# A new order of 33 transfers instead of 39, and the transposes of the last four tiles moved off TensorE, in a matmul with scale and add

## The chip, the cores and the metric

One core of a Trainium2 chip. The metric is the device time of one execution in microseconds; lower is better. Spans quoted from profiles are about 1.8 us shorter than the device time of the same run.

## The reference

```
x: (16, 512, 1024) float32, weight: (1024, 768) float32, add_value: (16, 512, 768) float32, scale = 0.1
out = (scale * matmul(x, weight) + add_value).astype(float32)
```

The 16 x 512 rows of x are 64 tiles of 128 rows. A tile of x has 0.524 MB, a tile of addend or output 0.393 MB, and all data together are 87.03 MB.

## The kernel before

One queue, issued from SyncE, carries every transfer in the order of `STREAM`. An entry is (kind, first tile, tiles): `x` loads rows of x, `w` weights, `a` addends, `o` stores output, `l` and `r` store the left and right columns of a tile.

```
STREAM = [
    ("x", 0, 3), ("w", 0, 2), ("w", 2, 2), ("w", 4, 2), ("x", 3, 1), ("w", 6, 2),
    ("a", 0, 3), ("x", 4, 4), ("a", 3, 1), ("a", 4, 4), ("x", 8, 4), ("x", 12, 4),
    ("x", 16, 4), ("a", 8, 8), ("x", 20, 4), ("x", 24, 8), ("o", 0, 8), ("a", 16, 8),
    ("x", 32, 8), ("a", 24, 8), ("a", 32, 8), ("x", 40, 8), ("o", 8, 8), ("x", 48, 8),
    ...
X_SLOTS = 16      # tiles of x in SBUF at a time
A_SLOTS = 32      # addend tiles; the output is made in place
```

x is needed transposed. Early tiles are cast on GpSimd and transposed on TensorE. For the tiles of `MOVED_ACT` and `MOVED_POOL`, ScalarE or GpSimd moves a pair of tiles in 16 casting copies, and VectorE turns the pair with one stream transpose. Four consecutive pairs (one x load of eight tiles) alternate between the two engines, so each engine moves two pairs per load.

```
MOVED_ACT = [14, 18, 22, 26, 30, 34, 38, 42, 46, 50, 54, 58]
MOVED_POOL = [16, 20, 24, 28, 32, 36, 40, 44, 48, 52, 56]
...
        elif op == "x":
            if last >= X_SLOTS:
                while done["cast"] <= last - X_SLOTS:
                    step()                       # emits the work that frees the slots
            nc.sync.dma_start(xs[:, k:k + n, :], rows(x_v, s, n))
```

The load of x32-39 overwrites the slots of x16-23, so its issue waits until the pairs 16, 18, 20 and 22 are moved. SyncE issues in order: while this entry waits, nothing behind it is issued.

## Time and profile before

| | before |
|---|---|
| device time, median of 4 runs | 210.12 us (209.95 to 210.92) |
| profiled span | 208.5 us |
| packets on the queue | 5616 |
| longest waits of the issuer | for ScalarE's moves, 90.1 us in five waits |

The prediction shows the main lines. The view of what the issuer waited for has three more. The columns are waiting engine and line, what it waited for, and then microseconds in total, times, and the longest.

```profile
SPq L258 <- ACT va L118: 90.1, 5, 22.0
SPq L264 <- DMA out_dram<-ao: 40.1, 4, 23.2
SPq L272 <- DVE ao L185: 21.7, 8, 6.9
```

The issuer waits nearly all the time.

### The profile page before, as it was taken

The numbers are of one execution on the slowest core, as the hardware profiler recorded it, in microseconds if no ns is written. First come the engines' busy times: TensorE is split into PE (matmuls) and PEld (weight loads), VectorE is DVE, ScalarE is ACT, GpSimd is POOL, SyncE is SP. The second block draws the span as 40 slices with busy tenths as digits, with TensorE's granted clock in tenths as the row PEclk, the third lists the DMA queues.
The fourth block names the chain that finished last, engine by engine and source line by source line (L and its number), as shares of the span: only waits on it lengthen the run. The fifth ranks groups of instructions, "written<-read, shape, count | busy, mean of one in ns | idle before, by whom it ended". The sixth has DMA issues, their size and how long they took to land.

```text
span 208.5 us, 2886 instructions
## 1 busy us (share of the span) xinstructions
PE 181.6 (87%) x1096; PEld 110.7 (53%) x1096; DVE 101.3 (49%) x111; ACT 129.0 (62%) x206; POOL 124.3 (60%) x199
## 2 busy tenths in 40 slices
PE   0599399980899997999999999999999999989960
PEld 0455256650466664566666666666666666656630
DVE  0536535511466514855655555555553685233330
ACT  2423000499959798599999999999999900003210
POOL 1310524379898980999998899999999960001000
PEclk9999889996589999999999999999999999999997
DMA  6999999999999999999999999999999999999995
GB/s 236 415 428 440 413 429 434 421 450 406 454 418 448 407 429 462 404 443 420 442 434 413 461 418 424 420 429 437 421 434 424 432 439 424 429 418 439 429 394 214
DMA packets 5629, 87.21 MB, mean 418 GB/s; under 512 B 624, under 2 KB 752, under 8 KB 2032
## 3 DMA queue, kind: packets, MB, share of 16 engines
q1 hardware_dynamic: 5616, 87.03, 98.2%
q8 instruction: 8, 0.13, 0.3%
q14 instruction: 5, 0.04, 0.0%
HBM read 61.87 MB, written 25.17 MB: 417 GB/s over the span
## 4 chain that ended last, share of the span: by engine, by line
DMA 75%; ACT 9%; PE 7%; DVE 3%; SPq 1%; issue 1%; DVEq 0%
DMA out_dram<-ao 35%; DMA ao<-in_add_value_dram 22%; DMA xs<-in_x_dram 13%; ACT va L118 9%; PE mm L177 6%; DMA ao<-in_weight_dram 5%; DVE ao L185 2%; DVE xt L126 1%; PE tp L156 1%; SPq L258 1%; SPq L99 0%; SPq L264 0%; SPq L272 0%; DVEq L185 0%
## 5 line engine op out<-in xcount | busy, mean ns | idle before, releaser
L177 PE MATMUL mm<-w_bf,xt 128*128 128x256 bf16 (+1 forms) x1024 | 173.8, 331 | 8.8 <-DVE xt L164 6.6
L177 PEld LDWEIGHTS <-xt 128*128 128x128 bf16 x1024 | 101.3, 99 | 76.9 <-DVE xt L164 7.0
L118 ACT CAST va<-xs 32x512 bf16<-32x512 f32 x192 | 118.2, 616 | 28.8 <-DMA xs<-in_x_dram 19.1
L118 POOL CAST va<-xs 32x512 bf16<-32x512 f32 x176 | 106.8, 607 | 15.9 <-DVE xt L126 6.2
L185 DVE SCALAR_TENSOR_TENSOR ao<-mm,ao 128x768 f32<-128x768 f32 (+2 forms) x62 | 58.1, 942 | 78.1 <-PE mm L177 49.1
L146 POOL CAST xb<-xs 128x1024 bf16<-128x1024 f32 x15 | 15.2, 1040 | 43.4 <-PE tp L156 22.5
L164 ACT COPY xt<-tp 128x512 bf16<-128x512 bf16 (+1 forms) x11 | 8.2, 785 | 35.3 <-PE tp L156 35.3
L126 DVE STREAM_TRANSPOSE xt<-va 128x1024 f32<-128x1024 f32 x23 | 28.4, 1234 | 0.0
L156 PE MATMUL tp<-identity,xb 128*128 128x128 f32 x72 | 12.9, 314 | 11.2 <-DVE xb L142 7.4
L156 PEld LDWEIGHTS tp<-identity,xb 128*128 128x128 f32 x72 | 9.8, 161 | 13.7 <-issue 7.6
L164 DVE COPY xt<-tp 128x1024 bf16<-128x1024 bf16 x10 | 6.9, 686 | 10.1 <-PE tp L156 10.1
L101 DVE CAST w_bf<-ao 128x768 bf16<-128x768 f32 x8 | 4.1, 556 | 3.8 <-DMA ao<-in_weight_dram 3.8
L142 DVE CAST xb<-xs 128x512 bf16<-128x512 f32 x3 | 1.9, 696 | 6.8 <-DMA xs<-in_x_dram 6.8
L144 POOL CAST xb<-xs 128x512 bf16<-128x512 f32 x2 | 1.6, 834 | 5.5 <-DMA xs<-in_x_dram 5.5
L144 ACT CAST xb<-xs 128x512 bf16<-128x512 f32 x1 | 0.6, 618 | 4.8 <-DMA xs<-in_x_dram 4.8
L213 DVE TENSOR_SCALAR ao<-mm 128x768 f32<-128x768 f32 x2 | 1.8, 952 | 1.9 <-PE mm L177 1.9
L245 DVE TENSOR_TENSOR ao<-ao 128x768 f32<-128x768 f32 x3 | 2.7, 951 | 0.0
L144 ACT ACT_TABLE_LOAD x1 | 1.3, 1283 | 0.7 <-PEq L289 0.7
L210 ACT ACTIVATE ao<-mm 128x768 f32<-128x768 f32 x1 | 0.8, 817 | 0.0
masks.py:197 POOL MEMSET identity<- 128x128 f32 x1 | 0.2, 204 | 0.3 <-POOLq L289 0.3
masks.py:199 POOL TENSOR_SCALAR_AFFINE_SELECT identity<-identity 128x128 f32<-128x128 f32 x1 | 0.3, 292 | 0.1
L289 POOL MEMSET const-float32-0.0<- 128x1 f32 x1 | 0.1, 98 | 0.2 <-issue 0.2
(3 smaller groups left out, 0.3 us busy)
## 6 DMA issues: line engine op xcount, KB each, us to landing
ao<-in_add_value_dram SPq DMA_DIRECT2D x7, 3072.0 KB, 26.1
out_dram<-ao SPq DMA_DIRECT2D x7, 3072.0 KB, 23.9
xs<-in_x_dram SPq DMA_DIRECT2D x5, 4096.0 KB, 18.8
xs<-in_x_dram SPq DMA_DIRECT2D x5, 2048.0 KB, 26.6
ao<-in_weight_dram SPq DMA_DIRECT2D x4, 768.0 KB, 9.6
xs<-in_x_dram SPq DMA_DIRECT2D x1, 1536.0 KB, 6.1
ao<-in_add_value_dram SPq DMA_DIRECT2D x1, 1536.0 KB, 19.3
out_dram<-ao SPq DMA_DIRECT2D x1, 1536.0 KB, 12.9
```

The lines of the kernel that those rows point to most:

```text
L101: nc.vector.tensor_copy(w_bf[:, j + i, :], ao[:, s + i, :])
L118: move(moved[t0][32 * b:32 * b + 32, :, a, :], src[32 * a:32 * a + 32, :, b, :])
L126: nc.vector.transpose(xt.rearrange("p i c m -> p (i c m)"), moved.pop(t0).bitcast(fp32).rearrange("p c a k -> p (c a k)"))
L142: nc.vector.tensor_copy(xb[:, 0:K // 2], src[:, 0:K // 2])
L144: other(xb[:, K // 2:K], src[:, K // 2:K])
L146: nc.gpsimd.tensor_copy(xb, src)
L156: nc.tensor.transpose(tp[:, c, :], pairs[:, c * P:(c + 1) * P], identity)
L164: evacuate(xt_tiles[t][:, c:c + q, :].bitcast(bf16), tp[:, c:c + q, :].bitcast(bf16))
L177: nc.tensor.matmul(mm_tiles[t, cols[0]][:, n0:n1], lhs(t, j), w_bf[:, j, n0:n1], start=(j == 0), stop=(j == KJ - 1))
L185: nc.vector.scalar_tensor_tensor(a, mm_tiles[t, part][:, n0:n1], float(scale), a, op0=mybir.AluOpType.mult, op1=mybir.AluOpType.add)
L245: nc.vector.tensor_add(ao[:, t, :], ao[:, EARLY_AT + t, :], ao[:, t, :])
L258: nc.sync.dma_start(xs[:, k:k + n, :], rows(x_v, s, n))
```

## The change

Its intent: fewer and larger transfers, no transposes on TensorE near the end, and a last store that waits for no arithmetic of its own. The diff, cut to its core:

```
     ("x", 0, 3), ("w", 0, 2), ("w", 2, 2), ("w", 4, 2), ("x", 3, 1), ("w", 6, 2),
-    ("a", 0, 3), ("x", 4, 4), ("a", 3, 1), ("a", 4, 4), ("x", 8, 4), ("x", 12, 4),
-    ("x", 16, 4), ("a", 8, 8), ("x", 20, 4), ("x", 24, 8), ("o", 0, 8), ("a", 16, 8),
-    ("x", 32, 8), ("a", 24, 8), ("a", 32, 8), ("x", 40, 8), ("o", 8, 8), ("x", 48, 8),
-    ("a", 40, 8), ("o", 16, 8), ("x", 56, 8), ("a", 48, 8), ("o", 24, 8), ("o", 32, 8),
-    ("a", 56, 8), ("o", 40, 8), ("o", 48, 8), ("o", 56, 4), ("o", 60, 1), ("o", 61, 1),
-    ("o", 62, 1), ("l", 63, 1), ("r", 63, 1),
+    ("x", 4, 4), ("a", 0, 8), ("x", 8, 8), ("a", 8, 8), ("x", 16, 8), ("a", 16, 8),
+    ("o", 0, 8), ("x", 24, 8), ("x", 32, 8), ("a", 24, 8), ("o", 8, 8), ("x", 40, 8),
+    ("a", 32, 8), ("o", 16, 8), ("a", 40, 8), ("x", 48, 8), ("x", 56, 8), ("a", 48, 8),
+    ("o", 24, 8), ("o", 32, 8), ("a", 56, 8), ("o", 40, 8), ("o", 48, 8), ("o", 56, 6),
+    ("l", 63, 1), ("r", 63, 1), ("o", 62, 1),
...
-MOVED_ACT = [14, 18, ..., 54, 58]
-MOVED_POOL = [16, 20, ..., 52, 56]
+MOVED_ACT = [14, 18, ..., 54, 58, 62]
+MOVED_POOL = [16, 20, ..., 52, 56, 60]
...
-        evacuate = nc.scalar.copy if t <= EARLY or t > LAST_PAIR else nc.vector.tensor_copy
+        evacuate = nc.scalar.copy if t <= EARLY else nc.vector.tensor_copy
```

The weight loads get another form of the same view, with the same rows.

More of the change, by code (lines that the diff above doesn't have):

```diff
@@ L26 @@
 EARLY = 3
-MOVED_ACT = [14, 18, 22, 26, 30, 34, 38, 42, 46, 50, 54, 58]
-MOVED_POOL = [16, 20, 24, 28, 32, 36, 40, 44, 48, 52, 56]
+MOVED_ACT = [14, 18, 22, 26, 30, 34, 38, 42, 46, 50, 54, 58, 62]
+MOVED_POOL = [16, 20, 24, 28, 32, 36, 40, 44, 48, 52, 56, 60]
 @with_exitstack
@@ L67, in rows @@
         return view[:, s // G, s % G:s % G + n, :]
-    w_v = weight.rearrange("(c p r) n -> p c r n", p=P, r=2)
+    w_v = weight.rearrange("(c p r) n -> p c (r n)", p=P, r=2)
     const = ctx.enter_context(tc.tile_pool(name="const", bufs=1))
@@ L95, in load_w @@
         s = A_SLOTS - KJ + j
-        if n == 1:
-            nc.sync.dma_start(ao[:, s, :], w_v[:, j // 2, j % 2, :])
-        else:
-            nc.sync.dma_start(ao[:, s:s + 2, :], w_v[:, j // 2, :, :])
+        assert j % 2 == n % 2 == 0
+        nc.sync.dma_start(
+            ao[:, s:s + n, :].rearrange("p (c r) n -> p c (r n)", r=2),
+            w_v[:, j // 2:(j + n) // 2, :])
         for i in range(n):
@@ L216, in head @@
             done["step"] = EARLY
-    LAST_PAIR = max(in_pair)
     EARLY_AT = A_SLOTS - KJ - EARLY
@@ L259 @@
             done["x"] = s + n
-            if last < EARLY:
+            if s < EARLY:
                 head(op, s, n)
```

## The prediction

> **What bounds the kernel now.** I read the page first, for the share of each engine and of the transfers (parts 1 to 4).
>
> ```profile
> PE 181.6 (87%) x1096; PEld 110.7 (53%) x1096; DVE 101.3 (49%) x111; ACT 129.0 (62%) x206; POOL 124.3 (60%) x199
> DMA  6999999999999999999999999999999999999995
> DMA packets 5629, 87.21 MB, mean 418 GB/s; under 512 B 624, under 2 KB 752, under 8 KB 2032
> q1 hardware_dynamic: 5616, 87.03, 98.2%
> ```
>
> All data move on one queue whose packets fill 98.2% of the 16 engines' time. Idle is 1.8% of 208.5 us = 3.75 us, and only the first and last slices are not full. To find what the busy time is worth, I asked for the windows (busy time of each engine, then PE clock, DMA share, GB/s):
>
> ```profile
> 4.00:16.00 12.00, 8.30 (x45) 5.57 (x46) 5.35 (x10) 3.74 (x7) 2.66 (x3) 1.00 1.01 420
> 88.00:156.00 68.00, 68.00 (x421) 40.96 (x420) 40.27 (x41) 66.25 (x108) 62.77 (x105) 1.00 1.00 430
> 198.00:205.00 7.00, 3.58 (x23) 1.90 (x20) 2.07 (x3) 0.73 (x1) 0.00 (x0) 1.00 0.96 398
> 205.00:206.00 1.00, 0.00 (x0) 0.00 (x0) 0.00 (x0) 0.00 (x0) 0.00 (x0) 0.80 0.72 280
> 206.00:207.00 1.00, 0.00 (x0) 0.00 (x0) 0.00 (x0) 0.00 (x0) 0.00 (x0) 0.50 0.34 124
> ```
>
> The long middle runs at 430 GB/s; the head with 6 KB rows at 420, the tail of one-tile stores at 398. 87.03 MB at 430 GB/s alone take 202.4 us of the 208.5 us. Only 6.1 us are start, small transfers and end together. So the kernel is bound by bytes on the transfer engines, and a change of order can win only out of those 6.1 us. Next the end of the chain of waits in order of time:
>
> ```profile
> 170.86 14.72 DMA ao<-in_add_value_dram
> 185.67 0.97 DVE ao L185
> 197.25 0.44 PE tp L156 x4
> 197.69 3.91 PE mm L177 x24
> 201.62 0.42 DVE ao L185
> ```
>
> From 186.7 us the chain runs through TensorE: the last tiles at 2.60 us each plus 0.44 us of PE transposes for tiles 60 to 63. But in those same microseconds the stores fill the transfer engines, and after the last finish at 202.04 us they still work at full share to 205. So TensorE and the transfers end nearly together, transfers last. Finally the timelines of GpSimd and the transfer issuer, which show who decides when the next x load may start:
>
> ```profile
> 43.98 2.55 POOL L118 CAST va<-xs 32x512 bf16<-32x512 f32 x4 [0.78 <-DMA xs<-in_x_dram]
> 46.60 1.03 POOL L146 CAST xb<-xs 128x1024 bf16<-128x1024 f32 x1
> 47.70 7.76 POOL L118 CAST va<-xs 32x512 bf16<-32x512 f32 x12
> 56.18 10.36 POOL L118 CAST va<-xs 32x512 bf16<-32x512 f32 x16 [0.72 <-DMA xs<-in_x_dram]
> 71.31 0.33 SPq L258 DMA_DIRECT2D xs<-in_x_dram  x1
> 95.98 0.33 SPq L258 DMA_DIRECT2D xs<-in_x_dram  x1
> 136.19 0.33 SPq L258 DMA_DIRECT2D xs<-in_x_dram  x1
> ```
>
> A pair of tiles costs GpSimd 10.4 us (16 moves) and ScalarE 10.03 us (the same view of it). An x load may start only when every tile in its slots has been moved; the waits view gives the issuer 90.1 us in five waits for ScalarE's moves. This is harmless as long as other transfers are still queued.
>
> **What the Trainium skill says.** (1) "DMA: Bandwidth & Descriptors", section "Where 436 GB/s comes from": the 16 SBUF ports carry 435 GB/s in all. The trace agrees: 430 in the middle, so there is nothing to gain per byte. (2) Same page, "Anatomy of one DMA": about 2.0 us fixed for a transfer plus its bytes, fitted there for GpSimd-issued transfers. Here the first x load ends its issue at 1.12 us and lands at 6.82 (first cast of VectorE); 5.70 less 1.573 MB / 430 GB/s = 3.66 leaves 2.04 us, so the trace agrees for SyncE's queue. (3) Same page, "Why a DMA increments its semaphore by 16 and not by 1": each engine ends its part with a semaphore write. The trace has 624 packets under 512 B = 39 transfers x 16. (4) "TensorE: Matmul & The Clock Gate", Part 1: idle time of about 3.4 us halves the clock. Between 52 and 56 us, after TensorE's idle stretch, the granted clock is 0.50.
>
> **The change part by part.**
> *Fewer transfers.* 39 become 33: a0-2, a3 and a4-7 become one (-2), x8 and x12 one (-1), x16 and x20 one (-1), o56-59, o60 and o61 one (-2). Packets are one per partition and transfer plus 16 semaphore writes, 144 x 39 = 5616, so I expect 144 x 33 = 4752. Estimated cost of a transfer: in the head 0.79 MB take 1.87 us at 420 and 1.83 at 430, 0.04 us; in the tail 7 us at 398 instead of 430 lose 0.5 us over five small stores, 0.1 us each. Saved: 4 x 0.04 + 2 x 0.1 = about 0.4 us, on the path, because the queue is the path. The weight view's new form moves the same 6 KB rows (the instruction order shows the same 128x1536 copies): nothing.
>
> *The head after the first six transfers.* a0-7 now comes as one 3 MB load after x4-7. By bytes it lands where a4-7 landed before (10.49 MB into the stream), about 28 us. VectorE's order has the three adds for tiles 0 to 2 (0.9 us each) before the copy of tile 4's transposes, so tile 4 starts at about 28 + 2.7 + 0.7 = 31.5 us instead of 28.2, and perhaps at half clock. Then a8-15 lands after 17.8 MB, about 47 us, instead of 51.3, and TensorE doesn't stand still until then. Both are off the path: TensorE is behind the transfers until the tail.
>
> *Tiles 60 to 63 off TensorE.* Removes 4 x 0.44 = 1.76 us of TensorE in the tail and four copies of 1.01 us on ScalarE; adds 16 moves to each of GpSimd (10.4 us) and ScalarE (10.0 us) and two transposes of 1.23 us to VectorE. TensorE's end was 201.6; GpSimd's twelve pairs now run nearly without a break, and its last ends about 188, so the turn of tile 60 frees it about 189 and five tiles of 2.6 us end near 200 to 201. The transfers end near 206.5 either way: about 0.
>
> *Tail order.* With l63 and r63 ahead of o62 the last issue waits for nothing of its own. o56-61 is issued at the finish of tile 61, about 196.5, while o48-55 lands about 200 (83.88 MB): still 3.5 us of work queued. Gain 0 to 0.3 us.
>
> **The rivals.**
> *A: the queue runs dry behind an x load.* Where the byte position of a landing is unchanged I read its time from the trace of before. x16-23 now lands as a whole at 22.0 MB, where x20-23 landed: 56.2. GpSimd's moves of pair 16, which waited until 44.0 for half of it, start only then, with the cast of tile 13 between them: 56.2 + 2.6 + 1.1 + 7.8, then pair 20: 10.4, gives 78.1; x32-39 is issued by 78.4. The transfer ahead of it, x24-31, lands at 80.85 (32.5 MB, where a16-23 landed). Lead 2.4 us. Likewise x40-47: 80.85 + 20.8 = 101.65, issued by 102.0, against o8-15 at about 105.2: lead 3.2. x56-63: 101.65 + 4 x 10.4 = 143.25, issued by 143.6, against x48-55 at 146.35: lead 2.75. Before, the first of these leads was 80.85 - 71.64 = 9.2 plus another load. A cold transfer needs 2.04 us, so none of the three runs dry, but by 0.4 to 1.2 us only. One GpSimd stall of 1 to 2 us ahead of 78 would cost as much: a time of 210.5 to 212. Against it: each lead is over 2.04 and the waits on buffers come out earlier than the moves.
> *B: TensorE sets the tail.* If removing 1.76 us of transposes were on the path, 208.4 us. Against it is the full share of the transfers from 186 to 205. If the new pace of GpSimd delays tile 60 by over 4 us, the stores wait instead: 211 to 213.
> *C: larger transfers run faster per byte.* If the pieces gave 1% more rate over the 11 MB concerned it would be 0.3 us; the 430 GB/s at the ports leaves no room for more.
>
> **Range and chances.** 210.14 - 0.4 (fewer transfers) - 0.2 (tail) + 0.3 (a chance of about one in three of a hole of 1 us) = 209.84, say 209.8 us. For 2% faster 4.2 of the 6.1 us of overhead would have to go, of which some 3 are start-up that isn't touched: 0.02. For 2% slower several holes are needed: 0.05. Range 208.8 to 211.3.
>
> **What would show it.** Right: 4752 packets on the queue, its share again 98% or more, 430 GB/s from 88 to 156 us, the x32-39 issue near 78, TensorE's last matmul near 200.5 with stores going on past 205. Wrong: a share clearly below 0.9 about 79 to 82, 104 or 146 us (rival A); a dip before 200 us in the stores (rival B); or a middle rate other than 430, which would break the sum at its root.

## The result, and the profile after

The changed kernel took 212.96 us (median of 4 runs, 212.49 to 213.59) against 210.12. The ratio is 1.0129, 95% interval 1.0092 to 1.0167. Ratios here are the mean time of one kernel's fast runs over that of the other's from the same rounds, so they are not quite the ratio of the medians. It is 2.8 us slower, clear of noise, and outside the predicted range of 208.8 to 211.3.

From the page of the changed kernel:

```profile
PE 180.7 (86%) x1080; PEld 109.0 (52%) x1080; DVE 102.0 (48%) x113; ACT 134.8 (64%) x218; POOL 130.0 (62%) x211
DMA  6999999999899998999999999999999999999994
DMA packets 4765, 87.21 MB, mean 413 GB/s; under 512 B 528, under 2 KB 656, under 8 KB 1552
q1 hardware_dynamic: 4752, 87.03, 97.8%
```

The packets are exactly the 4752 expected. The span is 2.6 us longer than before for the same bytes. Two slices of the busy row fell from 9 to 8: the eleventh (53 to 58 us) and the sixteenth (79 to 84 us). The first of them left no delay on most engines, as the table below shows. The timeline of GpSimd in the changed kernel, and after it that of the issuer:

```profile
55.81 2.55 POOL L117 CAST va<-xs 32x512 bf16<-32x512 f32 x4 [6.66 <-DMA xs<-in_x_dram]
58.43 1.03 POOL L145 CAST xb<-xs 128x1024 bf16<-128x1024 f32 x1
59.52 18.18 POOL L117 CAST va<-xs 32x512 bf16<-32x512 f32 x28
81.25 62.45 POOL L117 CAST va<-xs 32x512 bf16<-32x512 f32 x96 [3.54 <-DMA xs<-in_x_dram]
```

```profile
59.49 18.57 SPq L256 DMA_DIRECT2D xs<-in_x_dram  x2
78.11 0.42 SPq L262 DMA_DIRECT2D ao<-in_add_value_dram  x1
102.05 0.33 SPq L256 DMA_DIRECT2D xs<-in_x_dram  x1
```

GpSimd starts pair 16 at 55.8 instead of 44.0, finishes pair 20 at 77.7, and only then is x32-39 issued (the second of the two issues that the row from 59.49 merges, ending at 78.06). x24-31 has landed as a whole by 81.25. The prediction gave 78.1 for the moves and 80.85 for the landing. So the schedule was foreseen, and its cost was not. The windows of before (first three rows) and of the changed kernel, as in the prediction:

```profile
76.00:80.00 4.00, 4.00 (x27) 2.44 (x25) 0.00 (x0) 3.93 (x7) 1.58 (x3) 1.00 1.04 442
80.00:84.00 4.00, 2.81 (x18) 1.56 (x16) 3.12 (x4) 2.46 (x4) 0.91 (x2) 1.00 0.97 418
96.00:100.00 4.00, 4.00 (x27) 2.37 (x25) 2.15 (x3) 3.93 (x7) 3.70 (x8) 1.00 1.03 442
```

```profile
76.00:80.00 4.00, 4.00 (x27) 2.39 (x25) 2.26 (x3) 0.00 (x0) 1.62 (x3) 1.00 0.96 344
80.00:84.00 4.00, 4.00 (x27) 2.35 (x25) 3.63 (x4) 2.46 (x4) 2.58 (x5) 1.00 0.90 385
96.00:100.00 4.00, 4.00 (x20) 2.10 (x18) 0.76 (x2) 3.93 (x7) 3.74 (x7) 0.73 0.84 330
88.00:156.00 68.00, 63.37 (x380) 37.43 (x378) 35.74 (x36) 59.64 (x98) 58.47 (x97) 0.97 1.00 423
```

The last two numbers of a row are the transfer engines' busy share and GB/s. The rate falls to 344 and 385 about 80 us and to 330 about 98, and the whole middle is at 423 instead of 430. The share hardly shows it: from 78 to 81 us it reads 1.66, 0.43 and 0.76 in windows of 1 us, 0.95 on average. A slow packet counts as busy for its whole time. A packet's time and bytes are counted in the window where it starts, so short windows also scatter.

The trace also has what no view prints: for each transfer, the times at which the 16 engines each report the end of their part. I took the first, the ninth ("middle") and the last of the 16 (us from the start of the span), and the loss is the time since the same report of the transfer ahead, less bytes / 430 GB/s:

```
                issue   first   middle  last    lead to first   loss of the middle
before  a16-23  50.02   78.68   79.03   80.78
        x32-39  71.31   88.38   88.74   90.50    7.36           -0.04
        a24-31  71.69   95.68   96.08   97.80                    0.02
changed x24-31  59.49   78.67   78.87   81.13
        x32-39  77.73   89.46   89.87   90.89    0.94            1.25
        a24-31  78.11   97.64   97.88   99.73                    0.70
```

"Lead to first" is the time from the start of the issue until the first engine ends the transfer ahead. Engines do not end together. The last is 1.4 to 2.5 us behind the first here, and it alone decides when a consumer sees a transfer as landed (GpSimd starts on x24-31 at 81.25, just after the last report). When x32-39 was issued, the first engines had 0.9 us of work left. Eleven of the restart's 32 KB packets took 1.74 to 2.32 us; the median is 1.21. Then a24-31, which stands just ahead of the store o8-15, lost time as well. Middle-engine positions show where the 2.8 us came from: before the hole the changed kernel is 0.16 us ahead of before (78.87 against 79.03 after 32.5 MB), after x32-39 1.13 behind, after a24-31 1.80, after o8-15 2.13, and at the end 2.23. The last engine's final report is 2.55 us later (210.14 against 207.59).

The last engine, whose end sets the time, lost its 2.55 us elsewhere. It had 3.40 us of work left when x32-39 was issued, and x32-39 cost it 0.01 us. Its losses are 1.12 us at a16-23, the load ahead of the first store (it had been 0.36 ahead of before, 55.76 against 56.12 after 22 MB, and is 0.35 behind after x24-31), 1.52 at a24-31, the load ahead of the store behind the hole, and smaller ones later. So in this profile the hole reached the end of the kernel by way of the slow load behind it. (Neither the ninth nor the last report need always come from the same engine.)

### The profile page after: what moved, and what is told of

It reads as the page before. It is cut to its first block, busy times and chain, and to the rows that moved or that the text cites. A ratio compares the mean times of both kernels' runs of the same rounds, so it can differ in the third digit from the quotient of the medians.

```text
span 211.1 us, 2869 instructions
## 1 busy us (share of the span) xinstructions
PE 180.7 (86%) x1080; PEld 109.0 (52%) x1080; DVE 102.0 (48%) x113; ACT 134.8 (64%) x218; POOL 130.0 (62%) x211
## 3 DMA queue, kind: packets, MB, share of 16 engines
q1 hardware_dynamic: 4752, 87.03, 97.8%
## 4 chain that ended last, share of the span: by engine, by line
DMA 34%; PE 28%; POOL 25%; issue 6%; DVE 2%; SPq 1%; POOLq 0%; DVEq 0%
PE mm L176 26%; POOL va L117 24%; DMA xs<-in_x_dram 23%; DMA ao<-in_add_value_dram 11%; DVE ao L243 1%; PE tp L155 1%; POOL xb L145 1%; SPq L96 1%; DVE ao L184 1%; SPq L256 1%; DVE xt L163 0%; POOLq L117 0%; DVE xt L125 0%; POOLq L145 0%; DVEq L243 0%
## 5 line engine op out<-in xcount | busy, mean ns | idle before, releaser
L117 ACT CAST va<-xs 32x512 bf16<-32x512 f32 x208 | 128.1, 616 | 40.2 <-DMA xs<-in_x_dram 37.7
L117 POOL CAST va<-xs 32x512 bf16<-32x512 f32 x192 | 116.5, 607 | 23.9 <-DMA xs<-in_x_dram 15.5
L184 DVE SCALAR_TENSOR_TENSOR ao<-mm,ao 128x768 f32<-128x768 f32 (+2 forms) x62 | 56.8, 928 | 33.5 <-PE mm L176 18.3
L125 DVE STREAM_TRANSPOSE xt<-va 128x1024 f32<-128x1024 f32 x25 | 30.9, 1235 | 39.9 <-POOL va L117 39.9
L145 POOL CAST xb<-xs 128x1024 bf16<-128x1024 f32 x11 | 11.2, 1040 | 30.5 <-PE tp L155 19.3
L155 PE MATMUL tp<-identity,xb 128*128 128x128 f32 x56 | 10.2, 318 | 7.8 <-DVE xb L141 7.4
L155 PEld LDWEIGHTS tp<-identity,xb 128*128 128x128 f32 x56 | 7.7, 164 | 9.8 <-issue 7.7
L163 ACT COPY xt<-tp 128x512 bf16<-128x512 bf16 (+1 forms) x7 | 4.1, 656 | 8.5 <-PE tp L155 8.5
## 6 DMA issues: line engine op xcount, KB each, us to landing
xs<-in_x_dram SPq DMA_DIRECT2D x1, 2048.0 KB, 16.8
```

The lines of the kernel that those rows point to most:

```text
L117: move(moved[t0][32 * b:32 * b + 32, :, a, :], src[32 * a:32 * a + 32, :, b, :])
L125: nc.vector.transpose(xt.rearrange("p i c m -> p (i c m)"), moved.pop(t0).bitcast(fp32).rearrange("p c a k -> p (c a k)"))
L145: nc.gpsimd.tensor_copy(xb, src)
L155: nc.tensor.transpose(tp[:, c, :], pairs[:, c * P:(c + 1) * P], identity)
L163: evacuate(xt_tiles[t][:, c:c + q, :].bitcast(bf16), tp[:, c:c + q, :].bitcast(bf16))
L184: nc.vector.scalar_tensor_tensor(a, mm_tiles[t, part][:, n0:n1], float(scale), a, op0=mybir.AluOpType.mult, op1=mybir.AluOpType.add)
```

## The experiments

Theory, "late issue": an x load that is issued when its engines have less than about 2 us of work left restarts them cold, and the large early loads made x32-39 late. Rivals: the new tail and pairs, large transfers in themselves, and slow stretches of memory at random. Each run was timed in five rounds beside the kernel before.

### e1: x16-23 in two loads again

```
-    ... ("a", 8, 8), ("x", 16, 8), ("a", 16, 8),
+    ... ("a", 8, 8), ("x", 16, 4), ("x", 20, 4), ("a", 16, 8),
```

> Edit: x16-23 of the changed kernel in two loads of four tiles again. Theory 'late issue' (GpSimd starts pair 16 only when all of x16-23 is in, so x32-39 is issued at 77.7 us, 3.4 us before the last engine ends x24-31, and the queue restarts cold): GpSimd starts at about 50 instead of 55.8, x32-39 is issued at 72 to 73, no slow 32 KB packets at 79, the middle engine lands x32-39 near 88.7 instead of 89.87; time 211.3 to 212.0. Rival 'tail' (the six-tile store and the pairs taken off PE cost the time): 212.9. Rival 'chance of memory' (slow stretches come anywhere): 212.9, with slow packets elsewhere.

Measured 213.28 us, ratio 1.0145 (1.0124 to 1.0166). The time was missed. x32-39 was issued at 72.96 and lost 0.10 us, as the theory says, and a24-31 then lost nothing. But x40-47 was now issued at 102.25, 0.76 us before the first engine ran out (103.01), and lost 0.75. The next load ahead of a store, a32-39, lost 1.12. In the changed kernel x40-47 had a lead of 3.06 us only because the first hole had delayed the queue.

### e2: a24-31 ahead of x32-39

```
-    ("o", 0, 8), ("x", 24, 8), ("x", 32, 8), ("a", 24, 8), ("o", 8, 8), ("x", 40, 8),
+    ("o", 0, 8), ("x", 24, 8), ("a", 24, 8), ("x", 32, 8), ("o", 8, 8), ("x", 40, 8),
```

> Edit: a24-31 ahead of x32-39 in the order of the changed kernel, nothing else. Late issue: the queue has 7.3 us more work when x32-39 is issued at 77.7, so no hole at 79; x32-39 lands near 97.5, still ahead of GpSimd's need at 101.6; time 211.0 to 211.8. Rival 'tail': 212.9. Rival 'a load just ahead of stores is slow' (the slow 24 KB packets at 95 us): they disappear or move, as x32-39 now stands ahead of the store.

Measured 213.15 us, ratio 1.0143 (1.0120 to 1.0166). Missed for the same reason: x32-39 lost 0.11, but x40-47 (lead 0.59) lost 0.95 and a32-39 1.11. What follows from both is that the moving engines fix the issue times (102.3 in either), and repairing one hole brings the queue forward into the next.

### e3: pairs and tail of the change alone, in the kernel before

```
-    ("a", 56, 8), ("o", 40, 8), ("o", 48, 8), ("o", 56, 4), ("o", 60, 1), ("o", 61, 1),
-    ("o", 62, 1), ("l", 63, 1), ("r", 63, 1),
+    ("a", 56, 8), ("o", 40, 8), ("o", 48, 8), ("o", 56, 6), ("l", 63, 1), ("r", 63, 1), ("o", 62, 1),
(and the pairs 62 and 60 in the two MOVED lists)
```

> Edit: the kernel before with only the pairs 60 and 62 moved off PE and the new tail (six-tile store, tile 63 in two parts, tile 62 last); middle order of before. Late issue: x loads are issued as in before, 210.0 (209.7 to 210.4). Rival 'tail': 212 to 213, as the changed kernel.

Measured 209.97 us, ratio 0.9991 (0.9975 to 1.0008): the same as before. The tail and the pairs cost nothing, and gain nothing that can be measured.

### e4: the middle order of the change alone

The reverse: the changed kernel with the tail entries, the pairs and the evacuation rule of before.

> Edit: the changed kernel with the pairs and the tail of before, so only the order from the seventh transfer to o48-55 is new. Late issue: 212.7 to 213.1, as the changed kernel, with the same hole at 79. Rival 'tail': 210.

Measured 213.41 us, ratio 1.0155 (1.0129 to 1.0181). The whole loss is in the order from the seventh transfer to o48-55. (The new form of the weight loads is in this run too, but also in e5, which has little of the loss.) x32-39 had a lead of 0.67 and lost 1.36, and a24-31 1.07.

### e5: a whole addend load ahead of each late x load

```
-    ("o", 0, 8), ("x", 24, 8), ("x", 32, 8), ("a", 24, 8), ("o", 8, 8), ("x", 40, 8),
-    ("a", 32, 8), ("o", 16, 8), ("a", 40, 8), ("x", 48, 8), ("x", 56, 8), ("a", 48, 8),
+    ("o", 0, 8), ("x", 24, 8), ("a", 24, 8), ("x", 32, 8), ("o", 8, 8), ("a", 32, 8),
+    ("x", 40, 8), ("o", 16, 8), ("a", 40, 8), ("x", 48, 8), ("a", 48, 8), ("x", 56, 8),
```

> Edit: the changed kernel with an addend load of eight tiles ahead of each of x32-39, x40-47 and x56-63, so every late-issued x load finds over 7 us of work queued on even the fastest transfer engine. The first two edits showed the hole only moving from x32-39 to x40-47 (issued 102.3 while the fastest engine ended the load ahead at 103.0). Late issue, with the lead counted to the fastest engine: no hole at 79 nor at 103, and no slow 24 KB packets two transfers later; time 209.5 to 210.1 (before less the 0.4 us of saved packets). Rival 'eights are slow in themselves': 212.5 to 213.3 again.

Measured 210.65 us, ratio 1.0016 (1.0003 to 1.0028). It has the same 33 transfers, sizes, pairs and tail as the changed kernel, yet 2.3 us of the 2.8 are gone. Its windows:

```profile
76.00:80.00 4.00, 4.00 (x26) 2.44 (x25) 2.06 (x3) 0.00 (x0) 1.82 (x3) 1.00 0.87 373
80.00:84.00 4.00, 4.00 (x27) 2.36 (x26) 3.84 (x5) 2.46 (x4) 2.58 (x5) 1.00 1.04 449
96.00:100.00 4.00, 4.00 (x19) 2.06 (x17) 1.58 (x2) 3.93 (x7) 3.74 (x7) 0.69 1.04 444
```

Both dips are gone. The 373 from 76 to 80 are scatter ahead of 77 us: from 78 to 82, behind the place of the hole, e5 has 465 GB/s, the changed kernel 344 and before 434. By the reports a24-31 lost nothing and x32-39 0.01 us. TensorE waits 3.18 us up to 93.82 and runs at a low clock (0.69) from 96 to 100, much as in the changed kernel (3.34 us, 0.73). So TensorE's clock isn't what slowed the transfers there, and large transfers are not slow in themselves. The time is 0.5 us over the upper end expected: the middle engine ends 0.37 us ahead of before (206.25 against 206.62), but the last one 0.33 later (207.92 against 207.59). The last engine is behind as early as the landing of x24-31 (81.12 against 80.78), from a loss of 1.00 us at a16-23, the load ahead of the first store, that is not in before (-0.06; x24-31, which stands there in before, 0.37). Why is open.

### e6: another load between the hole and the store

```
-    ("o", 0, 8), ("x", 24, 8), ("x", 32, 8), ("a", 24, 8), ("o", 8, 8), ("x", 40, 8),
-    ("a", 32, 8), ("o", 16, 8), ("a", 40, 8), ...
+    ("o", 0, 8), ("x", 24, 8), ("x", 32, 8), ("a", 24, 8), ("a", 32, 8), ("o", 8, 8),
+    ("x", 40, 8), ("o", 16, 8), ("a", 40, 8), ...
```

> Edit: the changed kernel with a32-39 moved ahead of o8-15, so the hole at x32-39 stays, but two loads stand between it and the next store, and x40-47 has a full queue. Late issue: slow 32 KB packets at 79 as in the changed kernel (about 1.1 to 1.4 us on the middle engine). For the second loss (about 1.1 us at 95 us in the changed kernel): if it belongs to the switch from loads to stores, it moves to about 102 to 105, at the end of a32-39; if it follows the hole by a fixed time, it stays at 94 to 97. Time 212.3 to 213.0 either way; 211.3 if the second loss is gone.

Measured 215.37 us, ratio 1.0229 (1.0199 to 1.0259). x32-39 (lead 0.43) lost 1.59. The second loss moved with the switch to stores, as one of the two readings says: a24-31 lost nothing, a32-39 0.73. The windows of this run show it:

```profile
96.00:100.00 4.00, 4.00 (x18) 2.00 (x16) 0.73 (x1) 3.92 (x8) 3.74 (x7) 0.67 1.06 453
100.00:104.00 4.00, 4.00 (x26) 2.40 (x25) 2.71 (x3) 3.92 (x7) 3.72 (x7) 1.00 1.00 338
```

The time was missed because the order made another hole that I hadn't foreseen: x56-63 (lead 0.45) lost 1.34, and a48-55, ahead of the next store, 0.91.

### e7 and e8: two tiles, or one, ahead of x32-39 and x40-47

```
+    ("o", 0, 8), ("x", 24, 8), ("a", 24, 2), ("x", 32, 8), ("a", 26, 6), ("o", 8, 8),
+    ("a", 32, 2), ("x", 40, 8), ("a", 34, 6), ("o", 16, 8), ...
(e8: one tile and seven in place of two and six)
```

> Edit: the changed kernel with only a24-25 ahead of x32-39 and a32-33 ahead of x40-47 (0.79 MB, 1.83 us each). Lead to the fastest engine rises from 0.9 and 0.7 us to about 2.7 and 2.5 us, over the 2.04 us that a cold transfer needs. Late issue: no hole, 209.8 to 210.5 in spite of two transfers more. Rival 'a queue of a whole transfer is needed': a good part of the 3 us stays.

> Edit: the same with one tile ahead (0.39 MB, 0.91 us each): leads to the fastest engine about 1.8 and 1.6 us, just under 2.04. Late issue: a small hole of 0.2 to 0.5 us at each place, time 210.3 to 211.5. If the second loss follows any hole, it is there too, and the time is nearer 211.5.

e7 measured 213.52 us, ratio 1.0154 (1.0138 to 1.0171). The two places came out as expected: leads of 2.33 and 2.62, losses of 0.02 and 0.08. But x56-63, now with a lead of 0.55, lost 1.26 and a48-55 0.87, so the time was missed. e8 measured 213.88, ratio 1.0172 (1.0159 to 1.0185): x32-39 with a lead of 1.54 lost 0.56, and a25-31 behind it 1.18; x56-63 with 1.91 lost 0.48, and a48-55 0.59. The second loss was thus not in proportion to the hole.

### e9: two tiles ahead at three places

e7 with `("a", 48, 2), ("x", 56, 8), ("a", 50, 6)` in place of `("x", 56, 8), ("a", 48, 8)`.

> Edit: the changed kernel with two tiles of addend ahead of x32-39, x40-47 and also x56-63. The run with two tiles at the first two places had no hole there (leads to the fastest engine 2.33 and 2.62 us, nothing lost) but a new one at x56-63 (lead 0.55, 1.3 us lost and 0.9 at the next switch to stores). Late issue with the rule loss = 2.04 less the lead: leads over 2 everywhere, no hole, 210.3 to 210.9 as with whole loads ahead. If 213 again, the rule is wrong.

Measured 211.70 us, ratio 1.0066 (1.0050 to 1.0082). The leads were 2.37, 2.53 and 2.25 and the losses 0.31, 0.20 and 0.21, so the large holes are gone, though a lead just over 2 us isn't quite free. The time is 0.8 us over what was expected. In this profile the six-tile store was issued at 199.79, after the first engines had run out (199.04), and the middle one lost 0.92 there: a store that waited for arithmetic.

### e10: e5 with the six-tile store cut in four and two

> Edit: the version with whole addend loads ahead of the three x loads, and the six-tile store cut in four and two. There the six-tile store was issued at 197.2, 0.12 us before the fastest engine ran out, and that engine lost 1.1 us, the middle one nothing. Expected: the fastest engine's loss goes, the end is set by the slowest engine and hardly moves: 210.3 to 210.7, within 0.2% of before. If over 0.4 us come back, the tail had a share in the loss.

Measured 210.56 us, ratio 1.0007 (0.9994 to 1.0020), as expected: the first engine's loss of 1.09 us at that store became 0.00, and the time moved by a tenth, within noise.

### e11: the store directly behind the hole

```
+    ("o", 0, 8), ("x", 24, 8), ("x", 32, 8), ("o", 8, 8), ("a", 24, 8), ("a", 32, 8), ("x", 40, 8),
+    ("o", 16, 8), ("a", 40, 8), ("x", 48, 8), ("a", 48, 8), ("x", 56, 8),
```

> Edit: in the changed kernel x32-39 keeps its hole, the store o8-15 comes directly behind it, then a24-31 and a32-39; a48-55 is ahead of x56-63, so that there is one hole only. Late issue: 0.9 to 1.5 us lost at x32-39 by the rule. Second loss: if it needs an addend load at the switch to stores it is gone (211.0 to 211.8); if any switch after a hole has it, it is at the end of x32-39 itself, as 32 KB packets slowed near 88 (212 to 213).

Measured 214.10 us, ratio 1.0180 (1.0166 to 1.0193). x32-39 lost 2.49 us in all: packets slow at its start (76 to 80 us) and again at its end, from 84 to 92 us, just ahead of the store. So the second loss doesn't need an addend load; this reading was right. The time is 1.1 us over the range. o56-61 was issued at 202.14, when the first engine had been idle for 2.2 us, and the last engine lost 1.08 us there. It came so late because a24-31 landed 7.7 us later than in the changed kernel (107.4 against 99.7), and TensorE ended late.

### e12: one hole put into the kernel before

```
-    ("x", 32, 8), ("a", 24, 8), ("a", 32, 8), ("x", 40, 8), ("o", 8, 8), ("x", 48, 8),
+    ("x", 32, 8), ("a", 24, 8), ("x", 40, 8), ("a", 32, 8), ("o", 8, 8), ("x", 48, 8),
```

> Edit: the kernel before, with one swap in its order of transfers: x40-47 ahead of a32-39 instead of behind it. Nothing is added or removed. In before x40-47 is issued at 96.0 and the fastest engine ends a24-31 at 95.7, so after the swap the lead to it is about -0.3 us. Rule: 2.3 us lost at x40-47, and about 1 us more at the end of a32-39, the next switch to stores: 212.5 to 214. Rivals that blame large transfers, the six-tile store or the pairs off PE: 210.2, as none of them is in this kernel.

Measured 213.91 us, ratio 1.0179 (1.0165 to 1.0194), as expected. Two neighbours exchanged, with nothing added, cost 3.8 us. x40-47 was issued 0.45 us after the first engine had ended a24-31 and lost 2.26 on the middle engine; a32-39 then lost 1.03. The issuer's row of this run's timeline, and then its windows:

```profile
96.16 0.33 SPq L258 DMA_DIRECT2D xs<-in_x_dram  x1
```

```profile
96.00:98.00 2.00, 1.95 (x14) 1.21 (x14) 0.23 (x1) 1.95 (x4) 1.87 (x4) 1.00 0.89 266
98.00:100.00 2.00, 2.00 (x15) 1.22 (x13) 1.94 (x2) 1.96 (x4) 1.87 (x4) 1.00 0.67 287
114.00:116.00 2.00, 2.00 (x14) 1.20 (x13) 1.58 (x2) 1.97 (x4) 1.85 (x4) 1.00 1.06 295
```

The rate drops at the issue and again at the switch to the store, with TensorE at full clock and busy. None of the rivals' parts is in this kernel. Slow stretches that come at random fall out as well: in e1, e2, e5 and e12 the loss came, or stayed away, where the lead said.

The losses of x loads against their leads, all places with a lead under 2.7 us (middle engine; e11 is left out, as its loss holds both parts):

```
lead to first  -0.45   0.43   0.45   0.55   0.59   0.67   0.76   0.94     1.54   1.91
loss            2.26   1.59   1.34   1.26   0.95   1.36   0.75   1.25     0.56   0.48
run             e12    e6     e6     e7     e2     e4     e1     changed  e8     e8

lead to first   2.25   2.33   2.37   2.44   2.49   2.53     2.53   2.55   2.62
loss            0.21   0.02   0.31   0.31   0.10   0.73     0.20   0.01   0.08
run             e9     e7     e9     e1     e4     changed  e9     e2     e7
```

Under 2 us, lead and loss add up to 1.5 to 2.4 us. With the loss, too, taken on the first engine it is 1.70 to 2.38. The first transfer of each run, which finds an idle queue, needs 1.94 to 2.10 us beyond its bytes by the same measure. The six-tile store at the end pays less: in the eight runs where it came late (leads of -2.24 to 1.17) lead and loss on the first engine add up to 1.21 to 1.29. Over 2 us the loss is mostly small. The middle is the ninth report, which isn't always the same engine, so a single value is uncertain: in before, x56-63 with a lead of 8.00 also shows 0.27.

## Why the prediction was wrong

The prediction named the mechanism, as its rival A, found the three places, and gave them too little weight. Its steps:

- **Bytes set the time.** Right as a bound, and the middle rate of e5 and of before confirms it. The stated test ("a middle rate other than 430") failed in the changed kernel at 423, because of the holes.
- **39 to 33 transfers save 0.4 us.** About right for most engines, and hidden by the rest. Packets were exactly 4752. The middle engine was 0.16 us ahead of before just ahead of the first hole, and in e5, without holes, 0.37 at the end. The last engine gained 0.36 by 22 MB and lost more at a16-23, so no gain shows in the time.
- **The head.** Tile 4's products started at 31.28 (31.5 predicted), off the path as said.
- **Tiles 60 to 63 and the tail: no effect, gain 0 to 0.3 us.** The first is right, shown by e3 (ratio 0.9991). The times were too early: TensorE ended near 203.4, not 200 to 201, and o56-61 was issued at 199.19, not 196.5. Its landing of the middle engine was still on time (loss under 0.1).
- **Rival A: "A cold transfer needs 2.04 us, so none of the three runs dry".** This is the step that failed. The predicted issue times and the landing of x24-31 were right within 0.5 us (issues ended at 78.06, 102.38 and 144.05; x24-31 landed at 81.13). But the 2.4 us of lead ran to the landing that consumers see, which is the last engine's. The 15 others ended up to 2.46 us earlier. Against the first engine the lead was 0.94 us, and the loss 1.25. The term that was left out, the spread of the engines, stood in the prediction's own lines: shares of 0.72 and 0.34 in its last two windows say that some engines were done while others worked on (2.42 us between first and last by the reports). For the last engine alone the reading held (0.01 us lost at x32-39); it paid behind the hole, as the next point says.
- **A hole costs what it leaves idle.** The prediction counted "a hole of 1 us" once. Runs show a second loss of 0.6 to 1.2 us at the next switch from loads to stores (0.70 in the changed kernel's profile; 1.03 in e12). On the last engine it was 1.52 us in the changed kernel and 1.62 to 1.83 in e1, e2 and e4, where the hole itself cost that engine nothing; in e12 that engine lost 1.88 at the hole and 1.99 behind it. It was not foreseen. e6 and e11 show that it goes with the switch, and e1, e2 and e5 that the load ahead of the same store (o8-15) loses at most 0.11 us when no hole came before. Why the engines are slow there is open.
- **Rival B** (TensorE sets the tail) isn't needed for the loss: the last engine shows no gap in the tail of the changed kernel. It had a part in e1, e9 and e11 (0.41, 0.92 and 2.16 us of the middle engine at o56-61). **Rival C** found no support.

For x32-39 the root in the change is the merged load of x16-23: GpSimd starts pair 16 at 55.81 instead of 43.98, and e1, which cuts that load again, loses 0.10 us there. For x40-47, where e1 and e2 found the next hole, it is the distance between x loads. Between the end of x24-31 and the start of x40-47 the queue holds 16.8 MB in before (39 us at 430 GB/s), and 10.5 MB in the changed kernel (24.4 us). Two GpSimd pairs take 20.8 us of that and the spread 2.5, which leaves about 1 us; e1 and e2 measured 0.76 and 0.59.

No version tried beats before beyond noise. The best is e3, the same as before; the gain of the saved packets never reached the end.

## What to carry to other kernels

In a kernel bound by one transfer queue, work out for every transfer whose issue waits on compute how much work the first engine to finish still has at that moment, not the last one, and keep it above about 3 us (leads of 3.02 to 3.32 lost nothing here, leads of 2.25 to 2.62 up to 0.73). The share of busy transfer engines hides such a hole. GB/s in windows of some microseconds shows it, with scatter; the engines' end reports, set against bytes / 430 GB/s, gave the losses here. When one hole is mended, check the next, since the compute-bound issue times stay where they are and the queue moves towards them.

## What the Trainium skill lacked or had wrong

- "DMA: Bandwidth & Descriptors", "Anatomy of one DMA", has the fixed cost of about 2.0 us and puts most of it at completion. It doesn't say what a queue pays that restarts with other work just finished. Here lead and loss add up to 1.5 to 2.4 us, with packets of 1.74 to 2.32 us in place of 1.21 at the restart, and for a late store the sum on the first engine is 1.21 to 1.29.
- Same page, "Latency and other measured facts", tells of slower engines and gives as a best guess a cause that belongs to GpSimd-issued transfers alone. Here all transfers are SyncE's, and yet the last engine falls 1.1 to 1.5 us behind at x8-15 (x8-11 where that is the load) in every run, and the spread grows to 2.4 us in before and 2.9 us in the changed kernel. In before a 16 KB packet of the instruction queue took 1.06 us at 30.3, just ahead of it. That this is the cause is only inferred; packets of the same kind at 78.43 and 100.16 came without a step of the last engine (-0.06 and -0.02).
- No page has the slow end of a load ahead of a store after a hole: 0.6 to 1.2 us on the middle engine, 1.5 to 1.8 on the last one in the changed kernel, e1, e2 and e4; cause unknown.
